# Gate rows laid one behind the other, and a plain fp32 projection for 32 short-sequence tokens

## The chip, the core and the metric

One NeuronCore of one Trainium2 chip runs the kernel. TensorE (PE; its weight loads are listed as PEld) multiplies matrices, VectorE (DVE) and ScalarE (ACT) work on tiles of 128 partitions, GpSimd (POOL) mostly issues DMAs here, SyncE (SP) issues DMAs alone. The metric is the device time of one execution in microseconds; less is better.

## The reference

One layer of a hybrid decoder is computed for a prompt of 1024 tokens and for 8 short sequences of 4 new tokens each (32 tokens). Each token goes through attention and a state-space mixer, and then through `_peer`, a retrieval of single-neuron experts. The change lies in the work for `_peer`:

```python
def block(xb):                                   # PEER_HEADS 8, 128 keys, TOPK 16
    q = (xb @ wq).reshape(PEER_BLOCK, PEER_HEADS, 2, PEER_HALF)       # wq 1024 x 2048
    s = jnp.einsum('qhcd,ckd->qhck', q, keys)
    s1, i1 = lax.top_k(s[:, :, 0], PEER_TOPK)
    s2, i2 = lax.top_k(s[:, :, 1], PEER_TOPK)
    ...                                          # the 16 best of s1 + s2 give idx
    g = jax.nn.softmax(top, axis=-1)
    act = jax.nn.gelu(jnp.einsum('qhkd,qd->qhk', u_tab[idx], xb))
    return jnp.einsum('qhk,qhkd->qd', g * act, v_tab[idx])
```

Each token has 8 heads of 16 experts, 128 weights, each belonging to a pair of keys (i1, i2) out of 128 x 128 experts.

## The kernel before

The prompt's tokens are split in two. For the last 640 (five blocks of 128, `TD`) the kernel works over all 16384 experts densely: it builds a gate matrix of 128 x 128 weights for each token, which is zero but for the 128 chosen experts, stores it in DRAM as `g_d`, and later streams all of `peer_u` and `peer_v` through TensorE (class `Dense`, the dense stage). For the first 384 tokens and the 32 short-sequence tokens it gathers the chosen rows of `peer_u` and `peer_v` one after the other (class `Sparse`): an indirect DMA on GpSimd brings 128 rows of 1024 floats into a tile `pu` or `pv`, and VectorE reduces (`pu`, line 1349) or accumulates (`pv`, line 1361) it. There are five such tiles in a ring.

The gate matrices are built in steps of `GT` = 8 tokens, 80 of them (class `Gates`, lines 1204 to 1224). In a step VectorE writes `h2` (line 1211), a bf16 one-hot of the second key in the order [key, token], with the 8 tokens of a key side by side; `hv` (line 1212), its first `GV` = 5 tokens times their weights, in fp32; and `h1` (line 1213), the fp32 one-hot of the first key, in the order [token, key]. ScalarE writes `ha` (line 1215), the other three tokens times their weights, in the order [token, key]. TensorE multiplies `h1` by `hv` or `ha` of each token (line 1219; an fp32 multiply of 128 x 128 x 128, which the trace lists as two instructions), four tokens to a PSUM tile `gps`, and ScalarE copies each `gps` into `gbuf` (line 1220). Four steps fill a `gbuf`, which SyncE stores into `g_d`: 20 blocks. All these tiles and `gps` have two buffers. In the trace `h` stands for `h1` and `h2` alike, told apart by their lines.

The short sequences' 32 tokens pass through `score` (with `score_steps`, lines 1050 to 1106) while the gates are built. Their 2048 columns of `q` are done in 16 pieces `m` of 128. Each piece loads a part of `wq_d` (1 MB; a copy of `peer_wq` that an earlier stage stored as a high and a low part) over GpSimd's queue, keeps 128 x 128 of it in TensorE and streams the 32 tokens through it. `mm3` (lines 139 to 141) does that in three products of high and low parts, 24 instructions `rqn` a piece. ScalarE copies the piece out as `rqTn`, and a matmul `rscn` against the keys follows. After the last piece the 16 best of each head are searched on VectorE (`top16`), the pair search follows (`select`), and the gathers of these 32 tokens come last of all.

A function `rest` writes the program down in order: it takes one piece of `short`, then `GATES_AT_ONCE` = 2 gate steps, and so on; when `short` is at its end the rest of the gate steps follow, and then the dense stage. Every piece yields a number w (2.0 for a piece of `score_steps`, `GT` * 0.5 for a gate step), and a function `weave` adds a gathered row into the order, at a price of 1.5, whenever w times `PACE` = 0.3 has added up to it. The framework may hoist instructions within each engine's order; dependences through tiles hold them together.

Of the kernel before, what the change touches and what calls it, by code (L numbers as in the profile page):

```python
# [20 lines left out]
D = 1024  # L21
SEQ = 1024
# [150 lines left out]
def bc(ap, *shape):  # L173
    return ap.broadcast_to(list(shape))
# [76 lines left out]
def build(ctx, nc, tc, a):  # L251
# [109 lines left out]
    def rest():  # L361
# [688 lines left out]
def score_steps(nc, a, ident, xn_d, groups, tv, ti, tag, wq_d, wp, sp, pp, qb):  # L1050
    size = lambda b: 128 if b < NB else NS
    keys = wp.tile([128, 2, 128], F32, name="keys" + tag)
    nc.sync.dma_start(keys, a["keysT"])
    cols = []
    for g, (blocks, xt) in enumerate(groups):
        T = sum(size(b) for b in blocks)
        step = T // -(-T // 512)
        assert step * -(-T // 512) == T
        xh, xl = xt or (wp.tile([128, 8, T], F32R, name=f"rxh{tag}{g}"), wp.tile([128, 8, T], F32R, name=f"rxl{tag}{g}"))
        cols.append((blocks, T, step, xh, xl))  # L1060
        for i, b in enumerate(blocks):
            n = size(b)
            cs = slice(i * 128, i * 128 + n)
            xn = sp.tile([128, D], F32, name=f"rxn{b}", tag="raw")
            nc.sync.dma_start(xn[:n], xn_d[b * 128 : b * 128 + n, :])
            for h in range(2):
                tp = pp.tile([128, 4, 128], F32, name=f"rtp{b}_{h}", tag="q", bufs=qb)
                for k in range(4):
                    c = h * 4 + k
                    nc.tensor.transpose(tp[:, k, :n], xn[:n, c * 128 : (c + 1) * 128], ident[:n, :n])  # L1070
                split(nc, xh[:, h * 4 : h * 4 + 4, cs], xl[:, h * 4 : h * 4 + 4, cs], tp[:, :, :n])
    for m in range(16):
# [4 lines left out]
        for g, (blocks, T, step, xh, xl) in enumerate(cols):  # L1077
            qT = sp.tile([128, T], F32, name=f"rqT{tag}{g}_{m}", tag=f"qT{g}")
            for c0 in range(0, T, step):
# [3 lines left out]
                nc.scalar.copy(qT[:, cs], ps[:, :step])  # L1083
            full = [b for b in blocks if b < NB]
            for b0 in range(0, len(full), 4):
                part = full[b0 : b0 + 4]
                ps = pp.tile([128, 4, 128], F32, name=f"rsc{tag}{g}_{m}_{b0}", tag="sc")
                s = sp.tile([128, 4, 128], F32, name=f"rss{tag}{g}_{m}_{b0}", tag="s")
                for j, b in enumerate(part):
                    o = (b0 + j) * 128  # L1090
                    nc.tensor.matmul(ps[:, j, :], qT[:, o : o + 128], keys[:, c, :], start=True, stop=True)
                nc.scalar.copy(s[:, : len(part)], ps[:, : len(part)])
                for j, b in enumerate(part):
                    top16(nc, tv(b)[:, h, c], ti(b)[:, h, c], s[:, j, :])
            if NB in blocks:

                if m == 0:
                    pn = pp.tile([128, 2, 2, 128], F32, name="rscn", tag="scn")
                q = slice(h // 2 * 32, h // 2 * 32 + 32)
                nc.tensor.matmul(pn[q, h % 2, c, :], qT[:, T - NS : T], keys[:, c, :], start=True, stop=True)  # L1100
                if m == 15:
                    s = sp.tile([128, 2, 2, 128], F32, name="rssn", tag="s")
                    nc.scalar.copy(s, pn)
                    for j in range(4):
                        top16(nc, tv(NB)[:, j // 2, j % 2], ti(NB)[:, j // 2, j % 2], s[:, j // 2, j % 2])
        yield max(sum(x[1] for x in cols) * 0.0117, 2.0)

# [82 lines left out]
class Gates:  # L1190
# [11 lines left out]
    def run(self, tb):  # L1202
        nc, sp, pp, i1T, i2T, wT = self.nc, self.sp, self.pp, self.i1T, self.i2T, self.wT
        buf = sp.tile([128, 128, TBLK], F32, name=f"gbuf{tb}", tag="gbuf")
        for t0 in range(0, TBLK, GT):
            t = tb * TBLK + t0
            h1 = sp.tile([128, GT, 128], F32, name=f"h1_{t}", tag="h1")
            h2 = sp.tile([128, 128, GT], BF16, name=f"h2_{t}", tag="h2")
            hv = sp.tile([128, 128, GV], F32, name=f"hv_{t}", tag="hv")
            ha = sp.tile([128, GT - GV, 128], F32, name=f"ha_{t}", tag="ha")  # L1210
            nc.vector.tensor_tensor(h2, self.key, bc(i2T[:, t : t + GT].unsqueeze(1), 128, 128, GT), OP.is_equal)
            nc.vector.tensor_tensor(hv, h2[:, :, 0:GV], bc(wT[:, t : t + GV].unsqueeze(1), 128, 128, GV), OP.mult)  # L1212
            nc.vector.tensor_tensor(h1, bc(self.iota.unsqueeze(1), 128, GT, 128), bc(i1T[:, t : t + GT].unsqueeze(2), 128, GT, 128), OP.is_equal)
# [604 lines left out]
```

## Time and profile before

| what | value |
|---|---|
| median of three runs | 3620.98 us (3619.76 to 3624.33) |
| profiled execution | 3620.32 us, its span 3617.9 us |
| busy in the span: PE, PEld | 3347.4 us (93%), 2929.9 us (81%) |
| busy in the span: DVE, ACT, POOL | 2716.4 us (75%), 1156.2 us (32%), 1233.4 us (34%) |
| mean granted clock of TensorE | 0.944 of full speed |

A share of busy time is an average over a span that holds stages with different limits, from the projections at the start to the dense stage at the end. The rows further down therefore stand for stretches of the span, for single lines of the kernel, and for instants. TensorE runs at one of two clocks, 2.4 GHz (granted clock 1.0) or 1.2 GHz (0.5); a stretch's PEclk is the mean of what was granted in it.

### The profile page before, as it was taken

How to read it: one execution, taken by the hardware profiler on the slowest of the kernel's cores; microseconds unless marked ns; L12 is line 12 of the kernel's file. 1: busy time of each engine (PE TensorE's matmuls, PEld its weight loads, DVE VectorE, ACT ScalarE, POOL GpSimd, SP SyncE). 2: the span in 40 equal slices, each digit the busy share in tenths (PEclk: the TensorE clock that was granted, in tenths of full speed). 3: DMA queues.
4: the chain of work that ended last, by engine and by line, in shares of the span. 5: the costliest groups of instructions: out<-in, count | busy, mean ns of one | idle time of the engine just before them, and what ended most of it. 6: DMA issues, size and time to landing. Idle time of an engine off the chain costs nothing.

```text
span 3617.9 us, 52406 instructions
## 1 busy us (share of the span) xinstructions
PE 3347.4 (93%) x19464; PEld 2929.9 (81%) x19464; DVE 2716.4 (75%) x5777; ACT 1156.2 (32%) x2268; POOL 1233.4 (34%) x1044
## 2 busy tenths in 40 slices
PE   8899899999999634998799999999999999999999
PEld 7778687765799523987798898889988989998898
DVE  7674664434577998779688888888888888888884
ACT  4333454422322422456522121222222222222221
POOL 1020100000000104222155556555555556555551
PEclk9889799999999866778899999999999999999999
DMA  3335931143322207777899999999999999999992
GB/s 132 86 88 155 315 130 46 48 152 111 115 82 71 87 26 250 290 248 252 294 308 312 318 318 325 320 315 341 321 314 313 342 333 318 326 317 324 327 328 104
DMA packets 324606, 832.19 MB, mean 230 GB/s; under 512 B 36696, under 2 KB 150488, under 8 KB 313536
## 3 DMA queue, kind: packets, MB, share of 16 engines
q0 software_dynamic: 130608, 510.98, 39.9%
q1 hardware_dynamic: 92752, 247.75, 20.0%
q10 hardware_dynamic: 100992, 70.13, 6.7%
q8 instruction: 153, 2.51, 0.3%
q14 instruction: 101, 0.83, 0.1%
HBM read 734.44 MB, written 92.94 MB: 229 GB/s over the span
## 4 chain that ended last, share of the span: by engine, by line
PE 42%; issue 19%; POOL 13%; DMA 13%; DVE 11%; ACT 2%; SPq 0%; ACTq 0%; POOLq 0%; DVEq 0%
POOL pv L1335 9%; DMA pv<-in_peer_v_dram,idx 6%; POOL pu L1335 4%; PE gps L1219 4%; PE oz L1029 3%; DMA pu<-in_peer_u_dram,idx 2%; DVE pu L1349 2%; PE po L709 2%; PE s L688 2%; PE kk L139 2%; PE rqp L139 2%; PE rqp L140 2%; PE rqp L141 2%; PE kk L141 1%; PE kk L140 1%
## 5 line engine op out<-in xcount | busy, mean ns | idle before, releaser
L1335 POOL DMA_INDIRECT pu<-in_peer_u_dram,idx x384 | 522.6, 1361 | 618.3 <-DVE pact L1349 478.9
L1335 POOL DMA_INDIRECT pv<-in_peer_v_dram,idx x384 | 521.4, 1358 | 391.2 <-DVE pacc L1361 282.9
L139 PE MATMUL da<-xdh,uh 128*128 128x320 f32 x2048 | 636.8, 311 | 19.0 <-ACT ga L1292 18.7
L141 PE MATMUL da<-xdh,ul 128*128 128x320 f32 x2048 | 634.8, 310 | 2.3 <-DVE ul L129 2.3
L140 PE MATMUL da<-xdl,uh 128*128 128x320 f32 x2048 | 635.1, 310 | 0.0
L1361 DVE SCALAR_TENSOR_TENSOR pacc<-pv,pw,pacc 128x1024 f32<-128x1024 f32 x416 | 533.8, 1283 | 100.0 <-DMA pv<-in_peer_v_dram,idx 90.8
L1349 DVE CUSTOM_DVE_ANT_0 pu<-pu,pxn 128x1024 f32<-128x1024 f32 x416 | 496.7, 1221 | 90.2 <-DMA pu<-in_peer_u_dram,idx 82.5
L139 PEld LDWEIGHTS da<-xdh,uh 128*128 128x128 f32 x2048 | 387.1, 189 | 30.3 <-ACT ga L1292 23.5
L140 PEld LDWEIGHTS da<-xdl,uh 128*128 128x128 f32 x2048 | 387.1, 189 | 6.4
L141 PEld LDWEIGHTS da<-xdh,ul 128*128 128x128 f32 x2048 | 386.6, 189 | 6.3 <-DVE ul L129 2.8
L139 PE MATMUL dy<-vh,hh 128*128 128x512 f32 x768 | 302.5, 394 | 20.4 <-DVE yac L1308 20.4
L140 PE MATMUL dy<-vl,hh 128*128 128x512 f32 x768 | 299.8, 391 | 0.0
L141 PE MATMUL dy<-vh,hl 128*128 128x512 f32 x768 | 298.0, 390 | 0.0
L128 ACT CAST uh<-ur 128x1024 fp32r<-128x1024 f32 x128 | 134.5, 1051 | 394.3 <-PE da L140 391.3
L1292 ACT ACTIVATE ga<-da 128x320 f32<-128x320 f32 x256 | 110.0, 432 | 428.6 <-PE da L141 426.8
L1219 PE MATMUL gps<-hv,h 128*128 128x128 f32 x800 | 203.8, 415 | 23.8 <-DVE hv L1212 5.5
L128 ACT CAST vh<-vr 128x1024 fp32r<-128x1024 f32 x128 | 132.0, 1049 | 249.2 <-DMA vr<-in_peer_v_dram 180.0
L129 DVE TENSOR_TENSOR vl<-vr,vh 128x1024 fp32r<-128x1024 f32 x128 | 156.4, 1223 | 60.1 <-ACT vh L128 59.6
L1219 PEld LDWEIGHTS gps<-hv,h 128*128 128x128 f32 x800 | 168.8, 242 | 39.8 <-issue 16.4
L139 PE MATMUL dres<-vh,hh 128*128 128x512 f32 x512 | 200.5, 392 | 0.0
L140 PE MATMUL dres<-vl,hh 128*128 128x512 f32 x512 | 199.6, 392 | 0.0
L139 PEld LDWEIGHTS dy<-vh,hh 128*128 128x128 f32 x768 | 144.2, 188 | 54.5 <-DVE yac L1308 25.2
(528 smaller groups left out, 7148.1 us busy)
## 6 DMA issues: line engine op xcount, KB each, us to landing
ur<-in_ut_dram SPq DMA_DIRECT2D x128, 512.0 KB, 6.3
vr<-in_peer_v_dram SPq DMA_DIRECT2D x128, 512.0 KB, 6.5
g_d<-gbuf SPq DMA_DIRECT2D x20, 2048.0 KB, 7.6
gt<-g_d ACTq DMA_DIRECT2D x32, 1280.0 KB, 18.1
wq_d<-wq POOLq DMA_DIRECT2D x16, 1024.0 KB, 7.8
rwp<-wq_d POOLq DMA_DIRECT2D x16, 1024.0 KB, 5.1
rwn<-wq_d POOLq DMA_DIRECT2D x16, 1024.0 KB, 5.4
wqr<-in_peer_wq_dram SPq DMA_DIRECT2D x16, 512.0 KB
```

Source lines behind the costliest of these rows:

```text
L128: nc.scalar.copy(hi, raw)
L129: nc.vector.tensor_tensor(lo, raw, hi, OP.subtract)
L139: nc.tensor.matmul(out, ah, bh, start=(first and i == 0), stop=False)
L140: nc.tensor.matmul(out, ah, bl, start=False, stop=False)
L141: nc.tensor.matmul(out, al, bh, start=False, stop=(last and i == n - 1))
L688: nc.tensor.matmul(s[:, c0 : c0 + w], qT[:, h, :], kT[:, h, c0 : c0 + w], start=True, stop=c0 + w != nk)
L1029: nc.tensor.matmul(z[:n], cat[:, k, :n], w[:, k, hs], start=(k == 0), stop=(k == 7))
L1219: nc.tensor.matmul(ps[:, :, j - j0], h1[:, j], hv[:, :, j] if j < GV else ha[:, j - GV], start=True, stop=True)
L1292: nc.scalar.activation(ga[:, cs], ps[:, :HW], AF.Gelu_apprx_tanh)
L1335: self.nc.gpsimd.indirect_dma_start(out=r, out_offset=None, in_=self.a[table], in_offset=bass.IndirectOffsetOnAxis(ap=ix, axis=0))
L1349: nc.vector.tensor_tensor_reduce(ur, ur, xn, 1.0, 0.0, OP.mult, OP.add, act[:, s : s + 1])
L1361: nc.vector.scalar_tensor_tensor(acc, vr, w[:, s : s + 1], acc, OP.mult, OP.add)
```

## The change

Two parts of the kernel are edited.

First, `hv` gets the order [token, key] that `ha` and `h1` have. TensorE then reads the 128 floats of a token one behind the other; before, they lay 5 floats apart. VectorE's multiply writes `hv` in that order and reads `h2`, whose order stays, with a step of 8 bf16 values; before, it read runs of 5 neighbours.

Second, the short sequences get a function of their own, `score_short`. Per head (8 in place of 16 pieces) it loads 1 MB of `peer_wq` itself, keeps the 32 tokens' rows in TensorE and streams 256 columns of the weights in fp32 through them: 8 matmuls, 16 instructions. ScalarE copies the result, TensorE transposes it in two parts, ScalarE copies it again, and two matmuls with the keys follow. It yields 4.0 a head and 2.0 after the `top16` searches, which so form a step of their own. `score` and `score_steps` lose the cases for a short block.

```diff
-                yield from score(nc, tc, a, ident, xn_d, [([NB], None)], lambda b: tvn[:, 0], lambda b: tin[:, 0], "n", wq_d, 1, "right")
+                yield from score_short(nc, tc, a, ident, xn_d, tvn[:, 0], tin[:, 0], "right")
...
-            if NB in blocks:
-
-                if m == 0:
-                    pn = pp.tile([128, 2, 2, 128], F32, name="rscn", tag="scn")
-                q = slice(h // 2 * 32, h // 2 * 32 + 32)
-                nc.tensor.matmul(pn[q, h % 2, c, :], qT[:, T - NS : T], keys[:, c, :], start=True, stop=True)
-                if m == 15:
-                    s = sp.tile([128, 2, 2, 128], F32, name="rssn", tag="s")
-                    nc.scalar.copy(s, pn)
-                    for j in range(4):
-                        top16(nc, tv(NB)[:, j // 2, j % 2], ti(NB)[:, j // 2, j % 2], s[:, j // 2, j % 2])
-        yield max(sum(x[1] for x in cols) * 0.0117, 2.0)
+        yield sum(x[1] for x in cols) * 0.0117
+
+
+def score_short(nc, tc, a, ident, xn_d, tv, ti, side):
...
+            sp = es.enter_context(tc.tile_pool(name="rsn", bufs=2))
+            pp = es.enter_context(tc.tile_pool(name="rpn", bufs=1, space=PSUM))
...
+        for k in range(8):
+            nc.tensor.transpose(tp[:, k], xn[:, k * 128 : (k + 1) * 128], ident[:NS, :NS])
+        nc.scalar.copy(xT, tp)
+
+        pn = pp.tile([128, 2, 2, 128], F32, name="rscn", tag="scn")
+        for h in range(8):
+            w = sp.tile([128, 2, 8, 128], F32, name=f"rwn{h}", tag="w")
+            nc.gpsimd.dma_start(w, a["peer_wq"][2 * h : 2 * h + 2].rearrange("c p k n -> p c k n"))
+            ps = pp.tile([NS, 2, 128], F32, name=f"rqn{h}", tag="q")
+            for k in range(8):
+                nc.tensor.matmul(ps, xT[:, k], w[:, :, k, :], start=(k == 0), stop=(k == 7))
+            qs = sp.tile([NS, 2, 128], F32, name=f"rqsn{h}", tag="qs")
+            nc.scalar.copy(qs, ps)
+            tp = pp.tile([128, 2, NS], F32, name=f"rqtn{h}", tag="q")
+            for c in range(2):
+                nc.tensor.transpose(tp[:, c], qs[:, c], ident[:NS, :NS])
+            qT = sp.tile([128, 2, NS], F32, name=f"rqTn{h}", tag="qT")
+            nc.scalar.copy(qT, tp)
+            q = slice(h // 2 * 32, h // 2 * 32 + 32)
+            for c in range(2):
+                nc.tensor.matmul(pn[q, h % 2, c, :], qT[:, c], keys[:, c, :], start=True, stop=True)
+            yield 4.0
+        s = sp.tile([128, 2, 2, 128], F32, name="rssn", bufs=1)
+        nc.scalar.copy(s, pn)
+        for j in range(4):
+            top16(nc, tv[:, j // 2, j % 2], ti[:, j // 2, j % 2], s[:, j // 2, j % 2])
+        yield 2.0
...
-            hv = sp.tile([128, 128, GV], F32, name=f"hv_{t}", tag="hv")
+            hv = sp.tile([128, GV, 128], F32, name=f"hv_{t}", tag="hv")
...
-            nc.vector.tensor_tensor(hv, h2[:, :, 0:GV], bc(wT[:, t : t + GV].unsqueeze(1), 128, 128, GV), OP.mult)
+            nc.vector.tensor_tensor(hv, h2[:, :, 0:GV].rearrange("p i t -> p t i"), bc(wT[:, t : t + GV].unsqueeze(2), 128, GV, 128), OP.mult)
...
-                    nc.tensor.matmul(ps[:, :, j - j0], h1[:, j], hv[:, :, j] if j < GV else ha[:, j - GV], start=True, stop=True)
+                    nc.tensor.matmul(ps[:, :, j - j0], h1[:, j], hv[:, j] if j < GV else ha[:, j - GV], start=True, stop=True)
```

The edits also move instructions. In the rows below a name such as `h_336` is the tile of the step that begins with token 336 (so step 43 of 80), `gps_0` and `gps_4` are a step's two halves, and a number at a name's end only counts tiles; the line numbers of the changed kernel are 27 higher around the gates.

The first place is TensorE's order between two pieces of the short sequences' projection. Before, after the last of a piece's 24 instructions come two gate steps, and after the first of them the match with the keys:

```order
L139 MATMUL rqn_2_0_14175<-rxhn_13994,rwn_14172 128x32
L140 MATMUL rqn_2_0_14175<-rxln_13995,rwn_14172 128x32
L141 MATMUL rqn_2_0_14175<-rxhn_13994,rwn_14172 128x32
L1219 MATMUL gps_0_14212<-hv_14204,h_48_14202 128x128 x4
L1219 MATMUL gps_4_14218<-hv_14204,h_48_14202 128x128
L1219 MATMUL gps_4_14218<-ha_14205,h_48_14202 128x128 x3
L1100 MATMUL rscn<-keysn,rqTn_2_14174 32x128
L1219 MATMUL gps_0_14237<-hv_14229,h_56_14227 128x128 x4
L1219 MATMUL gps_4_14243<-hv_14229,h_56_14227 128x128
L1219 MATMUL gps_4_14243<-ha_14230,h_56_14227 128x128 x3
L139 MATMUL rqn_3_0_14256<-rxhn_13994,rwn_14253 128x32
L140 MATMUL rqn_3_0_14256<-rxln_13995,rwn_14253 128x32
```

In the changed kernel, from one head's projection to the next one's:

```order
L1117 MATMUL rqn_14146<-rwn_14144,rxTn 32x256 x8
L1246 MATMUL gps_0_14132<-hv_14124,h_40_14122 128x128 x4
L1246 MATMUL gps_4_14138<-hv_14124,h_40_14122 128x128
L1246 MATMUL gps_4_14138<-ha_14125,h_40_14122 128x128 x3
L1122 MATMUL rqtn_14157<-ident,rqsn_14155 128x32 x2
L1246 MATMUL gps_0_14177<-hv_14169,h_48_14167 128x128 x4
L1246 MATMUL gps_4_14183<-hv_14169,h_48_14167 128x128
L1246 MATMUL gps_4_14183<-ha_14170,h_48_14167 128x128 x3
L1127 MATMUL rscn<-keysn,rqTn_14160 32x128 x2
L1117 MATMUL rqn_14217<-rwn_14215,rxTn 32x256 x8
L1246 MATMUL gps_0_14202<-hv_14194,h_56_14192 128x128 x4
L1246 MATMUL gps_4_14208<-hv_14194,h_56_14192 128x128
```

A gate step now stands between a head's projection and its transposes, and another between the transposes and the keys; per piece or head there are two gate steps as before, but there are half as many pieces.

The second place is VectorE's order where the `top16` searches of the short sequences begin (`MAX tvn`). Before, they stand at the step of token 336:

```order
L1211 TENSOR_TENSOR h_336_15622<-gkey,i2T 128x1024
L1349 ISA pu_62_15593,pact_9466<-pu_62_15593,pxn_9464 128x1024
L1349 ISA pact_9466 128x1
L1212 TENSOR_TENSOR hv_15598<-h_328_15597,wT 128x640
L1213 TENSOR_TENSOR h_328_15596<-giota,i1T 128x1024
L1349 ISA pu_63_15618,pact_9466<-pu_63_15618,pxn_9464 128x1024
L1349 ISA pact_9466 128x1
L1183 MAX tvn<-rssn 128x8 x4
L1212 TENSOR_TENSOR hv_15623<-h_336_15622,wT 128x640
L1213 TENSOR_TENSOR h_336_15621<-giota,i1T 128x1024
L1211 TENSOR_TENSOR h_344_15644<-gkey,i2T 128x1024
L1184 MAX_INDEX tin<-tvn,rssn 128x8 x4
```

In the changed kernel they stand at the step of token 160:

```order
L1239 TENSOR_TENSOR hv_14619<-h_152_14618,wT 128x640
L1238 TENSOR_TENSOR h_160_14745<-gkey,i2T 128x1024
L1240 TENSOR_TENSOR h_152_14617<-giota,i1T 128x1024
L1376 ISA pu_45_14640,pact_9466<-pu_45_14640,pxn_9464 128x1024
L1376 ISA pact_9466 128x1
L1210 MAX tvn<-rssn 128x8 x4
L1239 TENSOR_TENSOR hv_14746<-h_160_14745,wT 128x640
L1240 TENSOR_TENSOR h_160_14744<-giota,i1T 128x1024
L1376 ISA pu_46_14766,pact_9466<-pu_46_14766,pxn_9464 128x1024
L1376 ISA pact_9466 128x1
L1238 TENSOR_TENSOR h_168_14770<-gkey,i2T 128x1024
L1211 MAX_INDEX tin<-tvn,rssn 128x8 x4
```

The searches, and the pair search behind them, moved ahead of 22 gate steps that they stood behind.

The third place is TensorE's order where the first matmuls of the dense stage (`da`) stand between the gate steps. Before, they come after the step of token 600:

```order
L1219 MATMUL gps_0_16451<-hv_16443,h_600_16441 128x128 x4
L1219 MATMUL gps_4_16457<-hv_16443,h_600_16441 128x128
L1219 MATMUL gps_4_16457<-ha_16444,h_600_16441 128x128 x3
L139 MATMUL da_0_16606<-xdh,uh_16593 128x320
L140 MATMUL da_0_16606<-xdl,uh_16593 128x320
L139 MATMUL da_320_16632<-xdh,uh_16593 128x320
L140 MATMUL da_320_16632<-xdl,uh_16593 128x320
L1219 MATMUL gps_0_16478<-hv_16470,h_608_16468 128x128 x4
```

In the changed kernel they come after the step of token 440:

```order
L1246 MATMUL gps_0_15624<-hv_15616,h_440_15614 128x128 x4
L1246 MATMUL gps_4_15630<-hv_15616,h_440_15614 128x128
L1246 MATMUL gps_4_15630<-ha_15617,h_440_15614 128x128 x3
L139 MATMUL da_0_16277<-xdh,uh_16264 128x320
L140 MATMUL da_0_16277<-xdl,uh_16264 128x320
L139 MATMUL da_320_16303<-xdh,uh_16264 128x320
L140 MATMUL da_320_16303<-xdl,uh_16264 128x320
L1246 MATMUL gps_0_15651<-hv_15643,h_448_15641 128x128 x4
```

The same four and their followers so moved ahead by 20 gate steps, from step 77 to step 57.

## Rows read from the trace of the kernel before

**Rows 1.** Stretches of the dense stage; columns are named in the first row.
```profile
core 0: us, PE busy (x) PEld busy (x) DVE busy (x) ACT busy (x) POOL busy (x), PEclk, DMA share, GB/s
1800.00:2400.00 600.00, 584.34 (x3258) 530.75 (x3257) 494.78 (x597) 146.97 (x214) 345.51 (x250) 0.99 0.92 316
3000.00:3617.90 617.90, 606.34 (x3365) 547.35 (x3364) 490.60 (x549) 146.83 (x214) 318.23 (x237) 1.00 0.84 292
```

**Rows 2.** One tile, `pv`: the instructions on it.
```profile
L1361 DVE SCALAR_TENSOR_TENSOR pacc<-pv,pw,pacc x416: 1272/1283/1344, 1890.3 to 3544.9; 128x1024 f32<-128x1024 f32 x139
```

**Rows 3.** Stretches of the gates, all engines.
```profile
1422.00:1783.00 361.00, 332.63 (x1752) 309.69 (x1752) 297.06 (x485) 200.83 (x426) 89.78 (x83) 0.80 0.74 265
1430.00:1460.00 30.00, 30.00 (x144) 29.07 (x144) 18.92 (x26) 12.38 (x27) 6.15 (x7) 0.54 0.56 192
1430.00:1627.00 197.00, 193.89 (x1054) 180.30 (x1053) 142.65 (x190) 98.18 (x214) 46.88 (x49) 0.77 0.73 264
1627.00:1760.00 133.00, 114.57 (x565) 106.56 (x566) 131.97 (x266) 87.40 (x183) 36.26 (x29) 0.84 0.74 259
```

**Rows 4.** Stretches, instructions on `hv` alone (PE, PEld, DVE), on `pu` alone (DVE, POOL).
```profile
1627.00:1760.00 133.00, 89.21 (x355) 74.12 (x356) 28.73 (x35) 0.84 0.74 259
...
1422.00:1783.00 361.00, 82.87 (x68) 81.82 (x69) 0.80 0.74 265
```

**Rows 5.** Waits, 1430 to 1783: total us, times, longest us.
```profile
DVE hv L1212 <- PE gps L1219: 42.2, 31, 4.4
...
DVE h L1213 <- PE gps L1219: 14.4, 21, 2.7
```

**Rows 6.** Timeline of TensorE: start us, us, instruction, idle time before it.
```profile
1388.27 3.62 PE L1029 MATMUL oz<-won,cat 128*32 128x512 f32 x8
...
1428.99 2.63 PE L1219 MATMUL gps<-hv,h 128*128 128x128 f32 x10 [2.48 <-DVE hv L1212]
1431.43 1.46 PE L1219 MATMUL gps<-ha,h 128*128 128x128 f32 x6
1432.55 0.37 PE L139 MATMUL rqn<-rxhn,rwn 128*128 128x32 f32 x1
...
1464.79 0.26 PE L141 MATMUL rqn<-rxhn,rwn 128*128 128x32 f32 x1
1464.90 2.53 PE L1219 MATMUL gps<-hv,h 128*128 128x128 f32 x10
1467.25 0.85 PE L1219 MATMUL gps<-ha,h 128*128 128x128 f32 x6
1468.03 0.41 PE L1100 MATMUL rscn<-keysn,rqTn 128*32 128x128 f32 x2
```

**Rows 7.** Groups of VectorE, 1420 to 1785: busy us, mean ns, idle before.
```profile
L1213 DVE TENSOR_TENSOR h<-giota,i1T 128x1024 f32<-128x1024 f32 x80 | 97.7, 1222 | 14.5 <-PE gps L1219 14.4
...
L1212 DVE TENSOR_TENSOR hv<-h,wT 128x640 f32<-128x640 bf16 x80 | 65.7, 824 | 42.2 <-PE gps L1219 42.2
```

**Rows 8.** Groups of ScalarE, whole span.
```profile
L1215 ACT ACTIVATE ha<-h,wT 128x128 f32<-128x128 bf16 x240 | 108.7, 520 | 7.7 <-PE gps L1219 4.8 <-DVE h L1211 2.9
...
L131 ACT ACTIVATE whi<-wr,vec 128x1184 fp32r<-128x1184 f32 x8 | 10.3, 1285 | 4.1 <-DMA wr<-in_w_in_dram 3.9
...
L131 ACT ACTIVATE w_uqh<-w_uqr,vec 128x384 fp32r<-128x384 f32 x6 | 3.6, 610 | 1.2 <-DVE h L1652 1.0 <-DMA w_uqr<-in_w_uq_dram 0.3
```

**Rows 9.** Timeline of VectorE in the second half.
```profile
1700.63 0.70 DVE L1211 TENSOR_TENSOR h<-gkey,i2T 128x1024 bf16<-128x1024 bf16 x1
1701.23 1.23 DVE L1213 TENSOR_TENSOR h<-giota,i1T 128x1024 f32<-128x1024 f32 x1
1702.37 1.23 DVE L1349 CUSTOM_DVE_ANT_0 pu<-pu,pxn 128x1024 f32<-128x1024 f32 x1
...
1703.51 0.83 DVE L1212 TENSOR_TENSOR hv<-h,wT 128x640 f32<-128x640 bf16 x1
```

**Rows 10.** Timeline of all engines, end of the stretch.
```profile
1773.27 0.83 DVE L1212 TENSOR_TENSOR hv<-h,wT 128x640 f32<-128x640 bf16 x1 [2.38 <-PE gps L1219]
...
1783.00 0.33 SPq L1223 DMA_DIRECT2D g_d<-gbuf  x1
```

More of the change, by code (lines that the diff above doesn't have):

```diff
@@ L1050, in score_steps @@
 def score_steps(nc, a, ident, xn_d, groups, tv, ti, tag, wq_d, wp, sp, pp, qb):
-    size = lambda b: 128 if b < NB else NS
     keys = wp.tile([128, 2, 128], F32, name="keys" + tag)
@@ L1055, in score_steps @@
     for g, (blocks, xt) in enumerate(groups):
-        T = sum(size(b) for b in blocks)
+        T = len(blocks) * 128
         step = T // -(-T // 512)
@@ L1061, in score_steps @@
         for i, b in enumerate(blocks):
-            n = size(b)
-            cs = slice(i * 128, i * 128 + n)
+            cs = slice(i * 128, i * 128 + 128)
             xn = sp.tile([128, D], F32, name=f"rxn{b}", tag="raw")
-            nc.sync.dma_start(xn[:n], xn_d[b * 128 : b * 128 + n, :])
+            nc.sync.dma_start(xn, xn_d[b * 128 : b * 128 + 128, :])
             for h in range(2):
@@ L1069, in score_steps @@
                     c = h * 4 + k
-                    nc.tensor.transpose(tp[:, k, :n], xn[:n, c * 128 : (c + 1) * 128], ident[:n, :n])
-                split(nc, xh[:, h * 4 : h * 4 + 4, cs], xl[:, h * 4 : h * 4 + 4, cs], tp[:, :, :n])
+                    nc.tensor.transpose(tp[:, k, :], xn[:, c * 128 : (c + 1) * 128], ident)
+                split(nc, xh[:, h * 4 : h * 4 + 4, cs], xl[:, h * 4 : h * 4 + 4, cs], tp)
     for m in range(16):
@@ L1083, in score_steps @@
                 nc.scalar.copy(qT[:, cs], ps[:, :step])
-            full = [b for b in blocks if b < NB]
-            for b0 in range(0, len(full), 4):
-                part = full[b0 : b0 + 4]
+            for b0 in range(0, len(blocks), 4):
+                part = blocks[b0 : b0 + 4]
                 ps = pp.tile([128, 4, 128], F32, name=f"rsc{tag}{g}_{m}_{b0}", tag="sc")
@@ L1106, in score_steps @@
-        yield max(sum(x[1] for x in cols) * 0.0117, 2.0)
+        yield sum(x[1] for x in cols) * 0.0117
+def score_short(nc, tc, a, ident, xn_d, tv, ti, side):
+    with ExitStack() as es:
+        with tc.using_default_side(side):
+            sp = es.enter_context(tc.tile_pool(name="rsn", bufs=2))
+            pp = es.enter_context(tc.tile_pool(name="rpn", bufs=1, space=PSUM))
+        keys = sp.tile([128, 2, 128], F32, name="keysn", bufs=1)
+        nc.sync.dma_start(keys, a["keysT"])
+        xn = sp.tile([NS, D], F32, name="rxnn", bufs=1)
+        nc.sync.dma_start(xn, xn_d[SEQ:NT, :])
+        xT = sp.tile([128, 8, NS], F32, name="rxTn", bufs=1)
+        tp = pp.tile([128, 8, NS], F32, name="rtpn", tag="q")
+        for k in range(8):
[24 more added lines that the diff above has]
+        yield 2.0
```

## Prediction

> **What bounds the kernel now.** I read the stretches first. From 1800 us to the end TensorE is busy 584 of 600 and 606 of 618 us at a granted clock of 0.99 to 1.00 [rows 1], and the gathered rows, the only other long stream there, are all added up by 3546 us, 72 before the span ends [rows 2]. So this dense stage is TensorE's, the change doesn't touch it, and it starts when the last gate block is stored. What the change can move is the stretch before it: 1422 to 1783 us, 361 us, in which 80 gate steps (8 tokens each), the 16 pieces of the short sequences' projection and 68 gathered rows run together [rows 3, 4].
>
> That stretch has two halves with different limits [rows 3]. From 1430 to 1627 TensorE is busy 193.9 of 197 us (granted clock 0.77) and VectorE 142.7. From 1627 to 1760 VectorE is busy 132.0 of 133 us, TensorE 114.6. Then 23 us of mixed tail. The waits say the same: in the whole stretch VectorE waits 42.2 us with `hv` and 14.4 us with `h` for TensorE to give back their buffers [rows 5]. VectorE's sum is 297 us busy of 361, 64 idle. Whoever reads TensorE's 93% on the page would book every saved TensorE microsecond; nearly half of the gate steps (35 of 80 `hv` run between 1627 and 1760 [rows 4]) stand where VectorE is the limit.
>
> **The change on TensorE.** A weighted row in `hv` is read with a step of 5 floats (20 bytes), one in `ha` lies contiguous; otherwise the matmuls are the same. From start to start: ten `hv` from 1464.90 to 1467.25 are 0.235 us apart, six `ha` from 1467.25 to 1468.03 0.130. Early in the stretch, where the granted clock is near half (1.2 GHz), `ha` is 0.187 apart and `hv` 0.244, hardly slower than later: `hv` is paced by reading the operand, not by the clock [rows 6]. With all rows contiguous, a step (10 + 6 instructions) falls from 3.13 to 2.08 us, 84 us over 80 steps.
>
> The short projection now streams 128x384 weight loads and 32 columns each: 384 instructions, 0.11 us apart at full clock [rows 6], 42 us. Afterwards there are 8 heads of 16 instructions with 32 stationary columns and 256 streamed ones. The nearest row has that shape with 512 columns: eight in 3.62 us, 0.45 each [rows 6], so I take 0.22: 3.6 us a head, 28 in all, at twice that if the clock is at half. Two transposes and four key matmuls a head (0.1 to 0.13 each) bring it to 4.3 us, 34 us. TensorE thus saves about 10 us here. Eight loads of 1 MB go out instead of 16, and the gathers queue behind them on POOL; VectorE's 132.0 busy us of 133 leave no wait for a gather to be saved, so I book nothing for that. ScalarE gets a few copies more; it is busy 201 of 361 us [rows 3].
>
> **The change on VectorE.** This is the term that decides. The multiply that writes `hv` now writes contiguously, but reads `h2` with a step of 8 bf16, 16 bytes, for each of its 640 elements. Before, it read runs of five neighbours at 0.824 us, and `h` takes 1.222 us for 1024 elements [rows 7]: both are 1.04 ns an element and about 0.16 us fixed, so 0.824 is the full rate. No VectorE row of this trace reads at such a step. The nearest is ScalarE's `ha`, which reads the very same `h2` at the same step: 0.520 us for 128 elements. Its contiguous relatives with a scale from a pointer take 0.610 us for 384 and 1.285 us for 1184 elements, a line with 0.844 ns an element that gives 0.394 us at 128 [rows 8]. The step costs 0.126 us over 128 elements, 0.98 ns each, 1.83 ns instead of 0.84.
>
> The bounds: below, nothing (0.824 stays; VectorE's 1.04 ns an element is already slower than what TensorE draws at its 20-byte step, 0.235 us for 256 elements); above, ScalarE's ratio of 1.83 to 0.84 on VectorE's 1.04 ns, 2.26 ns, which makes 1.61 us. A gain is excluded, since it is at full rate now. I take ScalarE's 1.83 ns as the time an element takes: 640 x 1.83 + 0.16 = 1.33 us, 0.50 more than now. If it is an addition (0.98 ns on top) it is 1.45, and 1.49 if the rate halves.
>
> The Trainium skill ("Vector Engine (DVE) Microarchitecture Reference", section 5.2, "Measured stream behaviour on trn2 (trn3 not measured)") speaks against the edit: a port streams at full rate only where consecutive elements come in runs of at least two adjacent 4-byte words; with one source hopping every element it gives 1.73 ns a column against 1.05, and 2.50 with both sources at a small step. By 1.73 an estimate for `hv` is 1.26 us and the sum below ends 5 us lower; by 2.50 it is 1.75 us, beyond the rival "dearer read", and the kernel would end near 3639.
>
> **The sum.** VectorE is busy 297 us between 1422 and 1783 [rows 3]. To that come 80 x 0.50 = 40 us, two gathered rows more in that part of the order (2.4), and the two splits of the short rows go (0.6): 339 us. What it idles: up to the last short head its order now holds 20 gate steps, not 42. For these it needs 20 x (0.60 + 1.24 + 1.14) + 18 rows x 1.14 = 80 us by start-to-start distances [rows 9] (`hv` 0.82 less the 0.08 by which neighbours overlap, plus 0.50), TensorE 18 x 2.08 + 34 = 72 us at full clock and 94 at the 0.77 of now. So it idles between nothing and 14 us there; I take 8. The other 60 steps are VectorE's alone: TensorE needs 2.1 us a step, 3.0 at half clock, VectorE 3.0 and 0.85 rows of 1.14, 4 us. At the end, from the last `hv` (1773.3) to the last block's store (1783.0) TensorE worked off four steps and the first dense matmuls [rows 10]; those dense matmuls now stand ahead of step 57 instead of step 77 of TensorE's order, and one step and two copies are left: 4 us. 339 + 8 + 4 = 351, against 361: 10 us less. The profiled run took 3620.3 us (span 3617.9), 0.7 below the median of 3621.0. So 3611 us for the median.
>
> **Rivals.** A difference of 0.2%, 7 us, is about what a measurement here can tell from none.
> *Likeliest, 0.55*: as above, `hv` 1.2 to 1.45 us, 3601 to 3621. Some six tenths of this are over 0.2% faster.
> *Free read, 0.14*: `hv` stays near 0.82. Then TensorE bounds the first part (idle 16), VectorE's 299 + 16 + 4 = 319, 42 less: 3579. For it: TensorE's port delivers a 20-byte step in 0.92 ns an element, less than VectorE's 1.04. Against: `ha` on the same data.
> *Dearer read, 0.20*: VectorE's 80 reads cost more than TensorE gives back. The gain is gone where `hv` passes 1.45 us (10 / 80 = 0.125 on top of 1.33); halved rate, 1.49, gives 3624, within 0.2%; at 1.61 it is 80 x 0.28 = 22 us more, less some 4 that idling gives back: 3629. For it: all 80 steps pay, but only the steps where TensorE is the limit gain.
> *Cold short path, 0.08*: each head's chain (projection, copy, transposes, copy, keys) leaves TensorE waiting for ScalarE, whose queue has gate work in front; the clock stays near half, as it did from 1430 to 1460 (0.54) with TensorE busy all the time [rows 3]. TensorE then needs 18 x 3.0 + 8 x 8.3 = 120 us for that part against VectorE's 80, idle 40 instead of 8: 3643, or 3627 if half of it. Against: the gates' matmuls now stream without stalls, and a gate step stands between each pair of dependent instructions.
> *TensorE bounds all of it, 0.01*: 84 + 10 us less, 3527; VectorE's 132 of 133 us excludes it.
> The rest, 0.02, is for what I don't see.
>
> **How the numbers follow.** Predicted 3611. The likeliest case alone is 3601 to 3621. The range reaches to the free read below and over the halved rate to the milder cold path above: 3578 to 3630. Faster: 0.34 of the likeliest, the free read 0.14 and the small rest, 0.50. Same: 0.21 of the likeliest and half of the dearer read, 0.31. Slower: the other half and the cold path, 0.19.
>
> **What would show it.** `hv` on VectorE at about 1.33 us (right), 0.82 or 1.5 and more (wrong, by that side). `gps<-hv` at the pace of `gps<-ha`, 0.13 us. VectorE near 99% busy from the last short head to the end of the gates, TensorE there 55 to 70%; no wait of `hv` for `gps` left. The last store of `g_d` near 1773, the dense stage as long as before. I am wrong if the first part lasts much over 95 us, if VectorE waits for gathers, or if the dense stage itself changes its length.

## The result and the profile after

The changed kernel takes 3596.3 us (median of 7 runs, 3583.5 to 3610.0), the kernel before in the same comparison 3624.3 (7 runs). The ratio is 0.9933, 95% interval 0.9914 to 0.9953: some 24 us faster (28 by the medians), where 10 were forecast. The profiled execution took 3583.5 us, its span 3581.7.

To compare the gate stretch of several kernels, I cut it at two points that all of them have: the start of the instruction `oxn` of the short block (the last VectorE work ahead of the short sequences' projection) and the last store of `g_d`. Cut so, the stretch of the kernel before reads (length, then busy time and count of PE, PEld, DVE, ACT, POOL, then PEclk, DMA share, GB/s):

```profile
1409.80:1783.00 373.20, 333.68 (x1754) 310.21 (x1754) 304.83 (x498) 201.36 (x428) 98.58 (x89) 0.79 0.74 265
```

And the changed kernel, the same stretch and below it its parts (up to the last short head, up to the first dense matmuls, the end) and the dense stage:

```profile
1407.00:1749.00 342.00, 230.77 (x1514) 200.87 (x1514) 337.21 (x496) 200.22 (x427) 141.26 (x81) 0.86 0.73 265
...
1420.00:1494.00 74.00, 69.90 (x464) 50.92 (x464) 74.00 (x91) 47.75 (x111) 35.32 (x25) 0.97 0.94 348
1494.00:1653.00 159.00, 93.23 (x612) 86.55 (x612) 159.00 (x280) 94.36 (x197) 60.38 (x31) 0.86 0.65 235
1653.00:1749.00 96.00, 65.69 (x428) 62.11 (x428) 93.22 (x110) 57.44 (x119) 35.73 (x19) 0.84 0.71 255
1749.00:3581.70 1832.70, 1791.43 (x9940) 1623.90 (x9940) 1496.32 (x1769) 445.25 (x643) 1023.88 (x747) 0.99 0.90 311
```

VectorE was busy 304.8 of 373.2 us and is busy 337.2 of 342.0. The dense stage (last row) has the length that it had, 1832.7 against 1783.0 to 3617.9, 1834.9. Everything that came before the stretch was 2.8 us shorter in this execution (1407.0 against 1409.8); over all profiled executions of the study the stretch starts between 1406.0 and 1415.2, and the dense stage lasts 1832.7 to 1850.6 us, so differences of a few microseconds there mean nothing. 31 of the 36 us between the two profiled spans lie in the gate stretch.

VectorE's groups there (busy us, mean ns of one, idle before), to be held against [rows 7]:

```profile
L1239 DVE TENSOR_TENSOR hv<-h,wT 128x640 f32<-128x640 bf16 x80 | 104.3, 1310 | 0.0
L1240 DVE TENSOR_TENSOR h<-giota,i1T 128x1024 f32<-128x1024 f32 x80 | 98.5, 1232 | 0.0
L1376 DVE CUSTOM_DVE_ANT_0 pu<-pu,pxn 128x1024 f32<-128x1024 f32 x73 | 89.7, 1232 | 0.0
L1238 DVE TENSOR_TENSOR h<-gkey,i2T 128x1024 bf16<-128x1024 bf16 x80 | 55.3, 700 | 0.0
```

`hv` takes 1310 ns in place of 824, and VectorE waits for TensorE no more: the waits of [rows 5] are gone. The only row of VectorE in the list of waits of this stretch is

```profile
DVE gkey L1227 <- DMA giota<-in_iota_dram: 2.0, 1, 2.0
```

TensorE's timeline at the beginning, against [rows 6]:

```profile
1424.77 1.38 PE L1246 MATMUL gps<-hv,h 128*128 128x128 f32 x10
1425.99 0.83 PE L1246 MATMUL gps<-ha,h 128*128 128x128 f32 x6
1426.76 1.91 PE L1117 MATMUL rqn<-rwn,rxTn 128*32 128x256 f32 x8
1428.60 1.38 PE L1246 MATMUL gps<-hv,h 128*128 128x128 f32 x10
1429.82 0.83 PE L1246 MATMUL gps<-ha,h 128*128 128x128 f32 x6
1430.58 0.31 PE L1122 MATMUL rqtn<-ident,rqsn 32*128 32x32 f32 x2
1430.82 1.38 PE L1246 MATMUL gps<-hv,h 128*128 128x128 f32 x10
```

Ten `gps<-hv` are 0.122 us apart (1424.77 to 1425.99), six `gps<-ha` 0.128: no difference is left, and a step takes 1.99 us. Eight instructions of the short projection take 1.84 us, 0.23 each, and two transposes 0.24. At the end, against [rows 10], four microseconds lie between the last `hv` and the last store, where there were ten:

```profile
1744.92 1.30 DVE L1239 TENSOR_TENSOR hv<-h,wT 128x640 f32<-128x640 bf16 x1
...
1749.03 0.32 SPq L1250 DMA_DIRECT2D g_d<-gbuf  x1
```

### The profile page after: what moved, and what is told of

Read it like the earlier page. It is cut to its first block, busy times and chain, and to the rows that moved or that the text cites. A ratio compares the mean times of both kernels' runs of the same rounds, so it can differ in the third digit from the quotient of the medians.

```text
span 3581.7 us, 51910 instructions
## 1 busy us (share of the span) xinstructions
PE 3245.7 (91%) x19224; PEld 2822.6 (79%) x19224; DVE 2747.9 (77%) x5775; ACT 1155.8 (32%) x2267; POOL 1287.2 (36%) x1036
## 4 chain that ended last, share of the span: by engine, by line
PE 49%; issue 17%; POOL 11%; DMA 11%; DVE 10%; ACT 1%; SPq 0%; ACTq 0%; POOLq 0%; DVEq 0%
POOL pv L1362 8%; DMA pv<-in_peer_v_dram,idx 5%; POOL pu L1362 4%; PE oz L1029 3%; PE da L139 3%; PE da L140 3%; PE da L141 3%; PE dy L139 2%; PE po L709 2%; PE dy L140 2%; PE dy L141 2%; PE s L688 2%; PE kk L139 2%; PE rqp L139 2%; PE rqp L141 2%
## 5 line engine op out<-in xcount | busy, mean ns | idle before, releaser
L1362 POOL DMA_INDIRECT pu<-in_peer_u_dram,idx x384 | 571.1, 1487 | 598.3 <-DVE pact L1376 471.6
L139 PE MATMUL dy<-vh,hh 128*128 128x512 f32 x768 | 304.8, 397 | 17.6 <-DVE yac L1335 17.5
L140 PE MATMUL dy<-vl,hh 128*128 128x512 f32 x768 | 301.9, 393 | 0.0
L1246 PE MATMUL gps<-hv,h 128*128 128x128 f32 x800 | 124.5, 310 | 98.1 <-DVE hv L1239 42.0
L1246 PEld LDWEIGHTS gps<-hv,h 128*128 128x128 f32 x800 | 110.0, 216 | 112.9 <-issue 67.4
L141 PE MATMUL dres<-vh,hl 128*128 128x512 f32 x512 | 186.7, 390 | 0.0
```

Source lines behind the costliest of these rows:

```text
L139: nc.tensor.matmul(out, ah, bh, start=(first and i == 0), stop=False)
L140: nc.tensor.matmul(out, ah, bl, start=False, stop=False)
L141: nc.tensor.matmul(out, al, bh, start=False, stop=(last and i == n - 1))
L1246: nc.tensor.matmul(ps[:, :, j - j0], h1[:, j], hv[:, j] if j < GV else ha[:, j - GV], start=True, stop=True)
L1362: self.nc.gpsimd.indirect_dma_start(out=r, out_offset=None, in_=self.a[table], in_offset=bass.IndirectOffsetOnAxis(ap=ix, axis=0))
```

## The experiments

All kernels were timed beside the kernel before in five rounds. "Stretch" is the one defined above, read from one profile each; "rest" is its length less VectorE's busy time; "gathers" is the time that GpSimd took to issue the 73 gathers in it. The medians are of 5 to 12 runs. The difference of two medians and the ratio can disagree by several microseconds (20 and 13 for `hv` alone); where they do, both are given.

| kernel | median us | ratio to before, 95% | stretch | VectorE busy | rest | gathers |
|---|---|---|---|---|---|---|
| before | 3621 to 3622 | | 373.2 | 304.8 | 68.4 | 89.5 |
| hv alone | 3601.6 | 0.9964 (0.9943 to 0.9986) | 350.1 | 338.5 | 11.6 | 133.2 |
| short alone | 3591.7 | 0.9923 (0.9902 to 0.9944) | 337.8 | 302.1 | 35.7 | 90.4 |
| short alone again | 3592.3 | 0.9929 (0.9905 to 0.9953) | 337.5 | 301.9 | 35.6 | 90.6 |
| changed, again | 3597.2 | 0.9941 (0.9921 to 0.9961) | 352.2 | 337.5 | 14.7 | 188.1 |
| changed, third | 3593.5 | 0.9939 (0.9914 to 0.9963) | 342.1 | 337.1 | 5.0 | 132.5 |
| changed, GV 4 | 3580.9 | 0.9893 (0.9872 to 0.9914) | 329.6 | 319.3 | 10.3 | 138.8 |
| changed, GV 3 | 3565.7 | 0.9833 (0.9808 to 0.9859) | 310.9 | 302.3 | 8.6 | 118.5 |
| changed, near read | 3568.5 | 0.9847 (0.9823 to 0.9870) | 313.5 | 300.7 | 12.8 | 92.9 |
| changed, scalar form | 3620.8 | 0.9995 (0.9979 to 1.0012) | 360.7 | 356.0 | 4.7 | 143.8 |
| short alone, GV 4 | 3577.3 | 0.9864 (0.9840 to 0.9888) | 324.3 | 291.3 | 33.0 | 89.8 |
| short alone, GV 3 | 3556.5 | 0.9840 (0.9813 to 0.9866) | 305.9 | 281.2 | 24.7 | 85.2 |

**One part each.** The theory (A) is that after the change VectorE's own work sets the stretch, and that both parts shorten it by taking TensorE out of VectorE's way. The rival is that one of them carries the gain. The layout of `hv` alone:

```diff
-hv = sp.tile([128, 128, GV], F32, ...)          # the short projection as before
+hv = sp.tile([128, GV, 128], F32, ...)
...
```

> Only the weighted rows' layout is changed (hv in the order token, key); the short sequences' projection stays as before, in 16 pieces. Theory A (after the change VectorE's own work sets the whole gate stretch, and each of the two edits does part): TensorE gets 84 us back, VectorE's multiply costs 1.31 us in place of 0.82, 39 us over 80 steps, and VectorE hardly waits; the gate stretch lasts within some 10 us of the changed kernel's, the time is about 3600 us, 20 to 25 below before. Rival B (the saving comes from the shorter projection, which ends at step 20 and not at step 42; the layout alone only swaps 42 us of waits for 39 us of slower reads): 3615 to 3624, within 0.2% of before.

```profile
1411.60:1761.70 350.10, 253.69 (x1754) 239.09 (x1754) 338.48 (x498) 199.37 (x428) 142.45 (x89) 0.83 0.77 281
```

3601.6 us in the median, 20 below before as A has it; by the ratio it is only 13 us less (5 to 21), between A and B. The stretch decides for A: it is 23 us shorter, and some 8 us from the changed kernel's. VectorE is at its limit here too (338.5 of 350.1), and its waits of `hv` for TensorE are down from 42.2 us [rows 5] to 4.9:

```profile
DVE hv L1212 <- PE gps L1219: 4.9, 6, 1.3
```

The short projection alone (`hv` keeps its old order):

```diff
-yield from score(nc, tc, a, ident, xn_d, [([NB], None)], ..., "n", wq_d, 1, "right")
+yield from score_short(nc, tc, a, ident, xn_d, tvn[:, 0], tin[:, 0], "right")
```

> Only the short sequences' projection is changed; hv keeps the order key, token, so TensorE reads it with a step of 5 floats. Theory A: VectorE's sum falls by the 39 us that the slower multiply costs. TensorE bounds the part up to step 20 (18 x 3.13 + 34 = 90 us at full clock), then VectorE the other 60 steps (60 x 2.49 + 51 x 1.14 = 208 us, against TensorE's 60 x 3.13 = 188): about 300 us with the tail against 327 now, so 3575 to 3585, faster than the changed kernel by some 15 to 20 us. Rival B2 (the layout carries the gain, and TensorE's strided reads hold the stretch at its old length): 3605 to 3620.

```profile
1414.40:1752.20 337.80, 297.62 (x1514) 256.78 (x1514) 302.05 (x496) 203.37 (x427) 96.33 (x81) 0.92 0.74 269
```

```profile
DVE hv L1239 <- PE gps L1246: 27.3, 19, 3.5
```

3591.7 us: B2 is out, and A's number too is missed by some 10 us. The first part went as said (first `hv` at 1428.2, the copy behind the last head at 1520.8, 93 us against 90), but for the other 60 steps, 231 us against 208, I had left out some 20 us that VectorE needs for the searches of the short sequences (the sum of their groups), and VectorE still waits 29 us for TensorE. With the layout on top, those waits go and 35 us of VectorE's work come: no gain is left. The shorter projection also moved the searches and the first dense matmuls ahead, halved the number of loads and went with a higher granted clock (0.92 against 0.79); which of these carries its 26 to 28 us was not separated. Since 3592 and 3597 are close, the pair was run again, side by side:

> The short projection alone, GV = 5, once more beside the changed kernel, since 3592 and 3597 were not told apart. Theory A': the layout brings nothing on top of the shorter projection; it trades 29 us of VectorE's waits for 32 us more of its work and longer gather issues: equal to the changed kernel within 7 us, on either side. Rival (the first comparison was an accident and the layout is worth its own 10 us): the changed kernel is lower by 7 us or more.

> The changed kernel beside it, with a third profile. Theory: 3590 to 3600, hv 1.31 us, and again gather issues on GpSimd of 3 us and more in the stretch (5.2 and 18.4 at most in the two profiles before, 2.0 without the step in VectorE's read). If they come from the step, the profile of the short projection alone has none over 2 us.

3592.3 and 3593.5 us. In two comparisons the short projection alone was as fast as both parts together, within what can be measured; the rival that grants the layout 10 us of its own is out. The stretch is 4.6 us shorter without the layout (337.5 against 342.1). As the last expectation has it, the long issues of gathers came again in the changed kernel's third profile (8.75 and 5.28 us), and with the short projection alone none was over 2 us once the gate steps ran; one of 4.33 us ahead of them has its like in the kernel before (4.75).

**VectorE's sum.** Fewer of a step's rows on VectorE, in the changed kernel:

```diff
-GV = 5
+GV = 4
```

> The changed kernel with GV = 4: VectorE weights four rows of a step, ScalarE the other four. Theory A (VectorE's own work sets the stretch): hv falls from 1.31 to about 1.08 us, 80 x 0.23 = 18 us less, the time falls by 15 to 20 us below the changed kernel's. Rival C (ScalarE or TensorE follow closely behind): ScalarE gets 80 x 0.52 = 42 us more on 200 of 330, TensorE waits for ha, and the time falls by less than 5 us or rises.

```profile
L1239 DVE TENSOR_TENSOR hv<-h,wT 128x512 f32<-128x512 bf16 x80 | 85.8, 1076 | 5.2 <-PE gps L1246 5.2
```

3580.9, 16 below the changed kernel timed beside it (3597.2). With `GV = 3`:

> The changed kernel with GV = 3: VectorE weights three rows of a step, ScalarE five. Theory A (VectorE's sum): hv falls to about 0.85 us, another 18 us below GV = 4 (3581), 3563. Rival C (ScalarE becomes the limit: 200 + 2 x 80 x 0.52 = 283 us of a stretch of some 310): VectorE waits for ha or TensorE for ha, and the time stays between 3575 and 3585.

```profile
L1239 DVE TENSOR_TENSOR hv<-h,wT 128x384 f32<-128x384 bf16 x80 | 67.0, 845 | 1.6 <-PE gps L1246 1.4
```

```profile
1415.20:1726.10 310.90, 215.82 (x1514) 186.94 (x1514) 302.34 (x496) 260.37 (x587) 124.59 (x81) 0.93 0.79 290
```

3565.7: another 15 (22 by the ratios, and the stretch is 18.7 us shorter), although ScalarE is now busy 260 of 311 us. The three sizes of `hv` (845, 1076, 1310 ns at 384, 512, 640 elements) lie on a line of 1.82 ns an element.

**The read's price.** The same instruction without the step (a part of its line):

```diff
-h2[:, :, 0:GV].rearrange("p i t -> p t i")
+h2.rearrange("p i t -> p (i t)").rearrange("p (t i) -> p t i", i=128)[:, 0:GV]
```

> The changed kernel, but VectorE's multiply reads the first 640 values of h2 one behind the other instead of with a step of 8; it so weights the wrong values (the second key's one-hot is mixed over tokens), all instructions and transfers stay. Theory A (the step costs VectorE 0.49 us a multiply, and the step alone): hv is back at 0.82 us, VectorE's sum falls by 39 us to about 298; now TensorE's 18 x 2.1 + 34 us and 62 x 2.1 us are shorter everywhere, VectorE still never waits, and the time falls by 30 to 40 us below the changed kernel's, to about 3560. Rival (the cost is the order in which hv is written or the weights' broadcast, not the read): hv stays near 1.3 us and the time at 3597. On GpSimd: in the changed kernel a gather's issue took 1.70 us in the median and up to 5 and 18 us, 1.15 and 2.0 before. If hv's strided read does that, it is back at 1.15; if it is VectorE without gaps, it stays.

```profile
L1239 DVE TENSOR_TENSOR hv<-h,wT 128x640 f32<-128x640 bf16 x80 | 65.5, 823 | 6.6 <-PE gps L1246 6.4 <-issue 0.2
```

```profile
1411.70:1725.20 313.50, 221.06 (x1514) 192.66 (x1514) 300.68 (x496) 199.06 (x427) 98.89 (x81) 0.90 0.79 289
```

`hv` is back at 823 ns, so it is the read and neither the order of writing nor the broadcast weights. The time is 3568.5, by the medians 25 to 29 us below the changed kernel's and by the ratios 31 to 34, at the lower end of A's 30 to 40: TensorE makes VectorE wait 7 us again. This kernel leaves out that each token's own values of `h2` are picked. One that picks them with such a read would need `h2` in the order [token, key] too; what writing `h2` would then cost was not measured.

**Another form of the work.** One instruction for each token's row, without `h2` and ScalarE's `ha` (`i2T` is kept in fp32 for it):

```diff
-nc.vector.tensor_tensor(h2, self.key, bc(i2T[...], 128, 128, GT), OP.is_equal)
-nc.vector.tensor_tensor(hv, h2[:, :, 0:GV].rearrange("p i t -> p t i"), ..., OP.mult)
+for j in range(GT):
+    nc.vector.tensor_scalar(hv[:, j], self.iota, i2T[:, t + j : t + j + 1], wT[:, t + j : t + j + 1], OP.is_equal, OP.mult)
...
```

> The changed kernel, but VectorE makes the weighted row of each of the 8 tokens in one instruction from the list of keys (equal to the token's second key, times its weight, both as scalars of a partition), contiguous; h2, and ScalarE's part, are gone. Theory A (VectorE's sum decides): 8 instructions of 128 x 128 fp32 at the 0.22 us, 0.13 from start to start, of the same form elsewhere are 1.1 us in place of 0.60 + 1.21, 50 to 55 us less, and 3540 to 3550. Rival (such an instruction with scalars from a pointer costs the full 128 x 1.04 ns and 0.16 us, 0.22 from start to start): 1.76 us, no change, 3595. Rival 2 (TensorE's 2.1 us a step now bounds): with 80 x 2.1 + 34 = 200 us against VectorE's 80 x 2.24 + 83 + 30 = 290 this does not happen.

```profile
1655.56 2.12 DVE L1236 TENSOR_SCALAR hv<-giota,i2T,wT 128x128 f32<-128x128 f32 x8
1657.60 0.27 DVE L1198 TENSOR_TENSOR eq<-eq 128x256 bf16<-128x256 bf16 x1
```

3620.8 us, all of the gain lost. My price was wrong, even the rival's: eight of them take 2.04 us from start to start (1655.56 to 1657.60), 0.255 each, in place of the 1.81 us that they replace. Theory A itself holds: against the changed kernel's first and third profile VectorE is busy 18.8 and 18.9 us more, and the stretch is 18.7 and 18.6 us longer.

**The better version.** If VectorE's sum decides and TensorE has room, the old order of `hv` is the cheaper one once VectorE has few rows to weight. The short projection alone with `GV = 4` and `GV = 3`:

> Only the short projection is changed, hv in the old order, and GV = 4: four rows strided in TensorE, four contiguous. Theory A: VectorE's hv 0.82 to about 0.69 us, 10 us less; TensorE 8 x 0.235 + 8 x 0.13 = 2.92 us a step instead of 3.13, 80 steps with 34 us for the short path 268 us; VectorE waits less than the 29 us of the kernel with GV = 5 (3592), and the time is 3575 to 3582, like the changed kernel with GV = 4 (3581). Rival (the reads with a step hold TensorE at the same pace, which bounds it): 3588 to 3592.

> Only the short projection is changed, hv in the old order, and GV = 3. Theory A (VectorE's sum decides wherever TensorE needs less than VectorE): a step is 0.60 + 1.14 + 0.48 us on VectorE, 178 us over 80, with 73 rows of 1.14 and some 30 us besides about 290; TensorE 6 x 0.235 + 10 x 0.13 = 2.71 us a step, 251 us with the short path; ScalarE 260 us. The stretch is 295 to 305 us against 311 of the new order with GV = 3 (3566): 3552 to 3562. Rival (the two chase each other: VectorE still waits 20 us with hv for TensorE's reads with a step, or ScalarE's 16 copies and 5 rows a step come late): 3566 to 3575.

```profile
1411.10:1717.00 305.90, 235.51 (x1514) 206.06 (x1514) 281.20 (x496) 258.12 (x587) 91.21 (x81) 0.96 0.82 297
```

3577.3 and 3556.5 us, both inside A's times (the stretch with `GV = 3`, 305.9, is just over its 305). The last is the fastest kernel of the study, 37 us below the changed kernel timed beside it (3593.5): VectorE is busy 281 of 306 us, ScalarE 258, TensorE 236, and VectorE's waits for TensorE are down to 14 us in all:

```profile
DVE hv L1239 <- PE gps L1246: 9.0, 10, 1.6
...
DVE h L1240 <- PE gps L1246: 5.3, 10, 0.6
```

**The spread.** The changed kernel's first seven runs lay 27 us apart.

> The changed kernel once more, for a second profile of it and more times, since its seven runs spread over 27 us (3583 to 3610) where those of before spread over 9. Theory A says nothing on the spread; if VectorE is busy without a gap in every execution of the gate stretch, the profile's stretch is again 327 us and the difference lies in another stage. Rival: VectorE waits in some executions for TensorE or for gathered rows, and the stretch itself is 10 to 25 us longer.

```profile
1410.20:1762.40 352.20, 238.33 (x1514) 208.21 (x1514) 337.53 (x496) 200.65 (x427) 194.11 (x81) 0.84 0.70 258
```

```profile
DVE pu L1376 <- DMA pu<-in_peer_u_dram,idx: 8.0, 1, 8.0
```

In this execution the stretch lasted 352 us and not 342, and 8.0 of the 10 are one wait of VectorE for a gathered row. GpSimd's timeline just ahead of it:

```profile
1549.53 8.62 POOL L1362 DMA_INDIRECT pu<-in_peer_u_dram,idx  x1 [0.30 <-issue]
1558.46 18.38 POOL L1362 DMA_INDIRECT pu<-in_peer_u_dram,idx  x1 [0.30 <-issue]
1577.15 0.94 POOL L1362 DMA_INDIRECT pu<-in_peer_u_dram,idx  x1 [0.30 <-issue]
```

One issue of a gather takes 18.38 us and ends at 1576.84. VectorE had worked without a gap until 1576.03, when it came to a row that was not there; the next four issues take 0.94 us each. The rest of the spread isn't explained by this, and it is no mark of the change: in the later comparisons the kernel before spread over 23 to 28 us itself, and kernels without the step in VectorE's read over 4 to 21 (near read 4, short alone 3583.6 to 3604.6). Part of it lies in the dense stage, which lasted 1850.6 and 1841.2 us in the two profiles of the short projection alone, and 1832.7, 1835.8 and 1842.7 in the three of the changed kernel.

## Why the prediction was right, and where its sizes were off

**The bound** was read rightly: the dense stage kept its length, and the time moved by what the gate stretch lost. The gain was 24 to 28 us where 10 were forecast; 3596 lies in the range of 3578 to 3630, but below the 3601 to 3621 that the likeliest case gave itself. Of the signs listed, VectorE was busy 252.2 of the 255 us from the last short head to the end of the gates (99%) and TensorE 62%, as said; the last store of `g_d` came at 1749 and not near 1773.

**TensorE's terms** were right for each instruction: 0.13 us with contiguous rows (0.122), 2.08 us a step (1.99), 0.22 us for one of the projection (0.23). The 10 us booked for the shorter projection were too few: TensorE's busy time in the stretch falls by 36 us with it alone (333.7 to 297.6) and by 23 on top of the layout (253.7 to 230.8), with a higher granted clock each time.

**The price of `hv`,** on which the sign hung, was forecast from ScalarE's row as 1.33 us and is 1.31; over three sizes 1.82 ns an element, against ScalarE's 1.83. The bounds of 0.82 and 1.61 and the rivals "free read" and "dearer read" so fall; the free read's price was had in the near read, which took 3568.5 where 3579 had been worked out. The reason given for the free read, 0.92 ns an element on TensorE, counts 256 elements for 0.235 us; the rows list 128 columns for each such instruction, and no run shows that it reads them twice. Counted once, that is 1.84 ns, next to ScalarE's 1.83 and VectorE's 1.82, and then it speaks against the free read. The Trainium skill's figure for one source that hops every element (1.73 ns a column; "Vector Engine (DVE) Microarchitecture Reference", section 5.2) is near the trace's 1.82, within 5%, though it was measured on 4-byte words that hop 4 KiB, and here 2-byte values lie 16 bytes apart. Its 2.50 for small steps on both sources is not what this read with a broadcast second source took.

**Two terms were mis-sized**, the idle time that is left and the added work, each by some 10 us and to the same side. The forecast was 42 us more work less 52 us of idle time, -10; the stretch of the profile has 32.4 more work less 63.6 idle, -31 (in the second execution 32.7 less 53.7, -21, in the third 32.3 less 63.4, -31). Some 2 us of the idle time that went are a wait for the list of keys ahead of the first step, which the forecast's 361 us did not hold.

**The idle time:** 12 us were to be left, 8 in the first part and 4 at the end; 3 were, all in the last part. I had kept 8 us of idling in the first part, because I let TensorE need up to 94 us there at the granted clock of 0.77 that the kernel before had. It was granted 0.97, needed less than VectorE, and VectorE was busy 74.0 of 74 us. Nothing remained of the 8.

**The work** grew by less than 80 times the longer instruction. The busy times of VectorE's groups, added up over the stretch, grew by 42.5 us (339.3 to 381.8), 38.6 of it in `hv`. But instructions that follow each other without a gap overlap by some 0.1 us ([rows 9] show it), and with the gaps gone there are more such pairs: 10.1 us of the 42.5 are covered so. Each wait that goes thus also gives back an overlap, and I had not counted that. That 42.5 is so near my 42 is in part luck: 2.4 of mine stood for two additional rows that don't exist (73 lie in the stretch before and after).

**The cold path** did not happen. From 1422 to 1437 the granted clock was 0.92 and then 1.0, with TensorE busy all the time, where the kernel before had 0.54 from 1430 to 1460 with TensorE just as busy [rows 3]:

```profile
1422.00:1437.00 15.00, 15.00 (x87) 9.89 (x86) 15.00 (x21) 8.33 (x20) 7.65 (x6) 0.92 0.84 294
1437.00:1457.00 20.00, 20.00 (x142) 15.47 (x141) 20.00 (x25) 13.22 (x32) 10.36 (x8) 1.00 0.96 353
```

With the short projection alone it was granted 0.92 over the stretch, in the kernel before 0.79. What TensorE did differs (32 columns streamed an instruction, or 256, and its operand's step), but hv alone has the short columns too and 0.83; whether the grant follows one of these or something else was not separated.

**What I did not see** is that the parts don't add up. Both go after the same 57 us of waits for TensorE [rows 5]: the layout alone takes away 52 of them, the short projection alone 27, both together all. By the ratios the layout alone gives 13 us, the short projection alone 26 to 28, both together 21 to 24; on top of the short projection the layout so buys nothing for 39 us of additional work on the engine that is the limit. The prediction booked the two parts together and never asked what the shorter projection is worth by itself.

## What to carry to other kernels

Two edits that remove the same wait must be priced each alone, before they are priced together: here the second one only paid its cost. Where an engine is the limit over a stretch, its busy time in the profile predicts the length (here to within 5 to 15 us for every version in which VectorE hardly waited), so move rows off it before you lay out data for its neighbour. An operand's step that one engine pays could here be priced from another engine's row on the same data, per element (1.83 and 1.82 ns).

## What the hardware showed beside

With the step in VectorE's read, GpSimd's issue of a gather takes longer. These rows are `pu` alone, DVE and POOL, over the stretch: of the changed kernel, of its second execution, of the near read, and of the short projection alone (the old order, VectorE idle 36 us).

```profile
1407.00:1749.00 342.00, 89.68 (x73) 135.20 (x73) 0.86 0.73 265
```

```profile
1410.20:1762.40 352.20, 89.72 (x73) 188.14 (x73) 0.84 0.70 258
```

```profile
1411.70:1725.20 313.50, 88.59 (x73) 92.92 (x73) 0.90 0.79 289
```

```profile
1412.00:1749.50 337.50, 88.45 (x73) 90.63 (x73) 0.93 0.75 269
```

73 issues take 135 and 188 us with the step and 93 and 91 without, and VectorE is busy 96% of the near read's stretch as well. So it is the form of VectorE's work and not only that it has no gaps. The scalar form, which has no such step, shows it too (143.8 us). The Trainium skill ("SBUF — State Buffer", section "Who interferes with whom") says that a VectorE instruction with two inputs in SBUF contends with a GpSimd instruction that reads SBUF. The 18.38 us issue, which ended 0.8 us after VectorE had run out of work, would fit that; but `hv` has two such inputs in both orders, and only one of them lengthens the issues. What makes the difference stays open. It showed as a wait of VectorE in one of the changed kernel's three profiled executions, 8 us where a gather came late.
